# A first SwiGLU phase on [high | low] products, and four megabytes of modulation moved into the first mixer

## The chip, the cores and the metric

The program runs on one core of a Trainium2 chip as one launch. The metric is the device time of an execution in microseconds (us). The kernel before takes 1054.62 us as the median of three runs (1054.45 to 1054.63).

## The reference

A decoder trunk of two layers, one sequence of 256 tokens, width 1024, all in float32. Each layer has three sub-layers, each with RMSNorm and a modulation (shift, scale, gate) that is computed from a vector c:

```
mod = silu(c) @ ada_w[l] + ada_b[l]          # 1024 -> 9216: sh, sc, gt of the three sub-layers
x += 1/2 * gt1 * SwiGLU(mod(rms(x)), ffn1_w_in[l], ffn1_w_out[l])        # 1024 -> 2 x 2816 -> 1024
h  = mod(rms(x)); proj = h @ mix_w_in[l]
x += gt2 * concat(attention(8 heads x 64), conv(256 channels, 31 taps), GLA(4 heads x 64)) @ mix_w_out[l]
x += 1/2 * gt3 * SwiGLU(mod(rms(x)), ffn2_w_in[l], ffn2_w_out[l])
SwiGLU(h) = (silu(h @ w_a) * (h @ w_b)) @ w_out
```

At 256 tokens the block-sparse attention is plain causal attention over one block.

## The kernel before

The activations lie transposed in SBUF: 128 partitions of the feature dimension, 256 tokens along the free dimension. The weights stream from HBM once, 250 MB, by one DMA queue (SyncE's) in pieces of about 1 MB into a ring of five slots (`raw`). A slot is used again when both readers of it are done.

To keep float32 accuracy each operand is taken as a sum of a high and a low part in the type fp32r. `split` (L316) makes the parts of a weight piece: ScalarE casts the raw tile to `wh` (L330), VectorE subtracts to get `wl` (L333). A product is wh x high + wh x low + wl x high, and there are two ways to issue it. `mm3` (L360) uses three matmuls of 256 columns. `mm2` (L366) uses one matmul of 512 columns for wh against the neighbours [high | low] and one of 256 columns for wl against high; its two halves of the accumulator have to be added afterwards. `product` (L605 calls it) does a 256-column weight piece with `mm3`; both output halves fit one PSUM bank. `product2` does it with `mm2`; it takes two PSUM banks and ends with a ScalarE copy (L540) and a VectorE addition (L541) for each of them.

The six phases are (layer, part): (0, 0) the first SwiGLU, until about 225 us of the span; (0, 1) the first mixer, until about 348; (0, 2) the second SwiGLU; and the same for layer 1, whose mixer has about 738 to 860. In the kernel before only phase (0, 0) uses `product`, the later SwiGLU phases use `product2`.

The modulation weights are another 72 pieces of 1 MB on the same queue and ring. `PLAN` (L48) spreads them over the phases: for each phase (m, tensor, lo, hi), that is m steps while its weight pieces lo to hi are split, `tensor` of them on TensorE and the others on VectorE. `piece_done` (L350) issues them. A VectorE step is a multiply-add of a 128 x 2048 tile with one activation per partition (L229 for the first of a group, L231). A group of steps ends with a sum over partitions by four TensorE products (`ada_sum`, L250), a copy, and transposes and additions (`ada_finish`, L262, L267). `AT_END` gives a step on TensorE (L222) near the end of a phase.

The mixer multiplies W_in in pieces (L362 to L364, L722 to L724), forms the gate product of the linear attention (L801), runs the convolution's 31 taps on VectorE (L756), and attends two heads at a time in `attend` (L845), four times. One such block is: six score products (L852), masked maxima on VectorE (L860, L864), exponentials on ScalarE with their sums (L384), reciprocals on VectorE (L870), scaling on ScalarE (L872), six transposes of the probabilities on TensorE (L875), copies on ScalarE (L876), and the products with the values (L882). Then come the linear attention's state products (L932, the state S on VectorE L938 and L943, L947, L950), W_out for the attention and the other heads (L977 to L979 with split weights, L974 with raw ones), and the residual.

The order of each engine's instructions is not that of the text: a list scheduler sorts the whole program at build time by its own estimates of durations, and engines then run their queues in that order. Matmuls of weight pieces that are ready are so put under the latency of a softmax.

Of the kernel before, what the change touches and what calls it, by code (L numbers as in the profile page):

```python
# [8 lines left out]
F32 = mybir.dt.float32  # L9
# [3 lines left out]
AF = mybir.ActivationFunctionType  # L13
# [4 lines left out]
P = 128  # L18
T = 256
# [25 lines left out]
TAPS = (4, 2, 4, 4, 4, 4)  # L45
ORDER = (0, 2, 6, 4)

PLAN = {None: (0, 0, 0, 1), (0, 0): (22, 0, 0, 30), (0, 1): (0, 0, 0, 1), (0, 2): (19, 0, 5, 28), (1, 0): (15, 0, 5, 28),  # L48
        (1, 1): (0, 0, 0, 1), (1, 2): (4, 0, 2, 14)}
AT_END = {(0, 0): 1, (0, 1): 1, (0, 2): 1, (1, 0): 1, (1, 1): 0, (1, 2): 0}  # L50
HOOKS = {(0, 1): (0, 1), (0, 2): (0, 1), (1, 0): (0, 1), (1, 1): (0, 1), (1, 2): (0, 1)}
# [8 lines left out]
def trunk_kernel(ctx: ExitStack, tc: tile.TileContext, x, c, positions, ada_w, ada_b, ffn1_norm, ffn1_w_in,  # L60
# [4 lines left out]
    ACT, DVE, PE, POOL = nc.scalar, nc.vector, nc.tensor, nc.gpsimd  # L65
# [8 lines left out]
    def nm(s):  # L74
        uid[0] += 1
        return f"{s}_{uid[0]}"
# [5 lines left out]
    def unit(shape, dt=F32, s="u"):  # L82
        return u2.tile(shape, dt, tag="u2k", name=nm(s))
# [266 lines left out]
    def piece_done():  # L350
# [3 lines left out]
        ada_due(True)  # L354
        m, tensor, lo, hi = PLAN[state["phase"]]
        at = lambda x: m * min(max(x - lo, 0), hi - lo) // (hi - lo)
# [26 lines left out]
    def act(*args, **kw):  # L383
        chained(ACT.activation(*args, **kw).ins)  # L384
# [135 lines left out]
    def product(w):  # L520

        wh, wl = w
        o = halves(wide())
        for k in range(KD):
            for s in range(2):
                cs = P * s, P * s + P
                mm3(o[:, s, :], wh(k, *cs), wl(k, *cs), high(k), low(k), k + s == 0, k + s == KD)
        return o
# [35 lines left out]
    def ffn(l, i, w_in, w_out, done, first=None):  # L564
        begin(l, i)
        wi = w_in[l].rearrange("(k p) (ab f) -> p k ab f", p=P, ab=2)
        gT = []
        ws = []

        pairs = (l, i) != (0, 0)  # L570

        def piece(n, ahead=0):

            while len(ws) <= min(n + ahead, KF - 1):
                m = len(ws)
                ws.append(split(wi[:, :, m % 2, T * (m // 2):T * (m // 2) + T], [KD, T], fine=m < 2))
            return ws[n]

        state["ahead"] = piece
        def gated(a):  # L580
            for s in range(2):
                g = unit([P, 2 * T], F32R, "g")
                split_out(a[:, s, :], g)
                gT.append(g)

        if first is None:
            piece(1)
            pps = [[wide(), wide()] for _ in range(2)]
            opening(l, i, ws, pps, {HOOKS[l, i][0]: mean_square, HOOKS[l, i][1]: spread})
        else:  # L590
            open_ws, opened, bias, small = first
            ws += open_ws
        for ch in range(KF // 2):
            if (l, i) == (0, 0) and ch in (2, 6):
                next(tables_rope)
            if (l, i, ch) == (0, 2, 3):
                use_small(1, *load_small(1))
            if first is not None and ch == 3:
                use_small(0, *small)
            if first is not None and ch < 2:  # L600
                if ch == 0:
                    continue
                pb = product(piece(3))
                b = bias()
                for s in range(2):  # L605
                    act(opened[0][:, s, :], opened[0][:, s, :], AF.Silu, bias=b[:, s:s + 1])
                    DVE.scalar_tensor_tensor(opened[0][:, s, :], opened[1][:, s, :], b[:, 2 + s:3 + s],
                                             opened[0][:, s, :], op0=ALU.add, op1=ALU.mult)
                gated(opened[0])
                a = opened[2]  # L610
                for s in range(2):
                    act(a[:, s, :], a[:, s, :], AF.Silu, bias=b[:, 4 + s:5 + s])
                DVE.tensor_mul(a, a, pb)
            elif ch == 0:
                (a, ba), (b, bb) = rms(pps[0]), rms(pps[1])
                wh, wl = piece(2)
                pp = [wide(), wide()]
                for k in range(KD):
                    for s in range(2):
                        cs = P * s, P * s + P  # L620
                        mm3(pp[s][:, 0:T + 2], wh(k, *cs), wl(k, *cs), hT[:, k, 0, :], hT[:, k, 1, :], k == 0,
                            k == KD - 1)
                third = rms(pp)
                piece(3)
                modulated(l, i)
                for s in range(2):
                    act(a[:, s, :], a[:, s, :], AF.Silu, bias=ba[:, s, :])
                    DVE.scalar_tensor_tensor(a[:, s, :], b[:, s, :], bb[:, s, :], a[:, s, :], op0=ALU.add,
                                             op1=ALU.mult)
            else:  # L630
                if ch == 1:
                    a, ba = third
                    for s in range(2):
                        act(a[:, s, :], a[:, s, :], AF.Silu, bias=ba[:, s, :])
                elif pairs:
                    a = product2(piece(2 * ch))
                    act(a, a, AF.Silu)
                else:
                    a = unit([P, 2, T], F32, "ab")
                    act(a, product(piece(2 * ch)), AF.Silu)  # L640
                DVE.tensor_mul(a, a, (product2 if pairs else product)(piece(2 * ch + 1)))
            gated(a)
        wo = w_out[l].rearrange("(k p) n -> p k n", p=P)
        late = []
        for grp2 in range(4):
            pp = [wide(), wide()]
            for k0 in range(0, KF, 8):
                n = min(8, KF - k0)
                wh, wl = split(wo[:, k0:k0 + n, T * grp2:T * grp2 + T], [n, T])
                order = [(k, j) for k in range(n) for j in range(2)]  # L650
                if grp2 == 3 and k0 + n == KF:
                    order.sort(key=lambda t: t[1])
                for k, j in order:
                    g = gT[k0 + k]
                    mm2(pp[j], wh(k, P * j, P * j + P), wl(k, P * j, P * j + P), halves(g), k0 + k == 0, k0 + k == KF - 1)
                while late:
                    done(late.pop(0))
                if grp2 == 3 and k0 == 8:
                    ada(AT_END[l, i])
                    if done is not emit:  # L660
                        done.last()
            for j in range(2):
                for o in (pp[j][:, T:2 * T], pp[j][:, 0:T]):
                    residual(o, l, i, 2 * grp2 + j)
                if l == NL - 1 and i == 2:
                    late.append(2 * grp2 + j)
                else:
                    done(2 * grp2 + j)
        while late:
            done(late.pop(0))  # L670
# [545 lines left out]
```

## Time and profile before

| | before |
|---|---|
| median of three runs | 1054.62 us |
| the profiled execution | 1054.1 us, span 1052.4 us |
| granted TensorE clock, mean | 0.998 |
| TensorE busy | 1033.0 us, 98%, 6844 matmuls |
| VectorE busy | 848.7 us, 81% |
| ScalarE busy | 597.7 us, 57% |
| DMA | 251.40 MB, mean 239 GB/s |

The span is that of the profile, the execution's own time is 1.7 us longer. Busy shares are means over stages of different kinds; which engine limits a stage is read from the table of stretches, in which the busy time of an engine stands against the stretch's length, and from what TensorE waited for. Matmuls overlap, so the time of one is taken between the starts of many.

### The profile page before, as it was taken

How to read it: one execution, taken by the hardware profiler on the slowest of the kernel's cores; microseconds unless marked ns; L12 is line 12 of the kernel's file. 1: busy time of each engine (PE TensorE's matmuls, PEld its weight loads, DVE VectorE, ACT ScalarE, POOL GpSimd, SP SyncE). 2: the span in 40 equal slices, each digit the busy share in tenths (PEclk: the TensorE clock that was granted, in tenths of full speed). 3: DMA queues.
4: the chain of work that ended last, by engine and by line, in shares of the span. 5: the costliest groups of instructions: out<-in, count | busy, mean ns of one | idle time of the engine just before them, and what ended most of it. 6: DMA issues, size and time to landing. Idle time of an engine off the chain costs nothing.

```text
span 1052.4 us, 17429 instructions
## 1 busy us (share of the span) xinstructions
PE 1033.0 (98%) x6844; PEld 908.9 (86%) x6844; DVE 848.7 (81%) x1408; ACT 597.7 (57%) x1061; POOL 21.8 (2%) x58
## 2 busy tenths in 40 slices
PE   6999999999999999999999999999999999999998
PEld 5799998888888988888889888888879889888887
DVE  3798788879996899998669999866899779866652
ACT  4555454458667665564457555544767666555431
POOL 6000000001000000000000000000000000000000
PEclk9999999999999999999999999999999999999999
DMA  9999999985344679999666999867443455865430
GB/s 310 376 341 351 315 312 313 329 293 168 127 149 146 221 241 330 356 329 309 234 200 228 314 334 316 289 202 236 126 156 121 161 166 195 282 200 185 156 119 20
DMA packets 177638, 251.40 MB, mean 239 GB/s; under 512 B 7493, under 2 KB 156520, under 8 KB 170388
## 3 DMA queue, kind: packets, MB, share of 16 engines
q1 hardware_dynamic: 176480, 249.97, 70.5%
q8 instruction: 53, 0.87, 0.3%
q0 software_dynamic: 960, 0.28, 0.2%
q14 instruction: 29, 0.24, 0.1%
q10 hardware_dynamic: 116, 0.05, 0.0%
HBM read 249.23 MB, written 1.05 MB: 238 GB/s over the span
## 4 chain that ended last, share of the span: by engine, by line
PE 90%; ACT 3%; DVE 3%; DMA 3%; issue 0%; SPq 0%
PE mm L368 36%; PE mm L369 18%; PE mm L362 7%; PE mm L363 7%; PE mm L364 7%; PE mm L974 3%; PE mm L724 2%; PE mm L723 2%; PE mm L722 2%; DMA held<-in_ffn_w_in_dram 1%; ACT wh L330 1%; DMA adaraw<-in_ada_w_dram 1%; PE tp L222 1%; DVE wl L333 1%; PE tp L250 1%; DVE ab L756 1%
## 5 line engine op out<-in xcount | busy, mean ns | idle before, releaser
L333 DVE TENSOR_TENSOR wl<-raw,wh 128x1024 fp32r<-128x1024 f32 (+1 forms) x344 | 384.0, 1128 | 111.6 <-ACT wh L330 105.5
L330 ACT CAST wh<-raw 128x1024 fp32r<-128x1024 f32 (+1 forms) x344 | 330.9, 973 | 203.7 <-PE mm L368 100.9
L368 PE MATMUL mm<-hT,wh 128*128 128x512 f32 x912 | 322.8, 397 | 0.0
L369 PE MATMUL mm<-hT,wl 128*128 128x256 f32 x912 | 256.4, 282 | 0.0
L368 PE MATMUL mm<-g,wh 128*128 128x512 f32 x704 | 249.4, 398 | 0.0
L368 PEld LDWEIGHTS mm<-hT,wh 128*128 128x128 f32 x912 | 172.5, 189 | 43.0 <-DVE g L695 1.7
L369 PE MATMUL mm<-g,wl 128*128 128x256 f32 x704 | 197.6, 281 | 0.0
L362 PE MATMUL mm<-hT,wh 128*128 128x256 f32 (+1 forms) x656 | 188.4, 287 | 1.7 <-ACT wh L330 1.6
L363 PE MATMUL mm<-hT,wh 128*128 128x256 f32 (+1 forms) x656 | 187.2, 285 | 0.1
L364 PE MATMUL mm<-hT,wl 128*128 128x256 f32 (+1 forms) x656 | 186.6, 285 | 0.0
L369 PEld LDWEIGHTS mm<-hT,wl 128*128 128x128 f32 x912 | 171.8, 188 | 0.2
L368 PEld LDWEIGHTS mm<-g,wh 128*128 128x128 f32 x704 | 132.2, 188 | 35.0 <-ACT wh L330 2.5
L369 PEld LDWEIGHTS mm<-g,wl 128*128 128x128 f32 x704 | 133.0, 189 | 0.0
L362 PEld LDWEIGHTS mm<-hT,wh 128*128 128x128 f32 x656 | 125.2, 191 | 4.8 <-ACT wh L330 2.3
L231 DVE SCALAR_TENSOR_TENSOR adaacc<-adaraw,cact,adaacc 128x2048 f32<-128x2048 f32 (+1 forms) x59 | 123.5, 2093 | 3.9 <-DMA adaraw<-in_ada_w_dram 3.8
L363 PEld LDWEIGHTS mm<-hT,wh 128*128 128x128 f32 x656 | 124.9, 190 | 1.1 <-DVE hT L448 0.3
L364 PEld LDWEIGHTS mm<-hT,wl 128*128 128x128 f32 x656 | 124.9, 190 | 0.4 <-DVE wl L333 0.2
L540 ACT COPY ab<-mm 128x256 f32<-128x256 f32 x114 | 41.6, 369 | 51.5 <-PE mm L369 51.3
L546 DVE SCALAR_TENSOR_TENSOR xT<-mm,gate,xT 128x256 f32<-128x256 f32 x80 | 34.6, 478 | 25.1 <-PE mm L369 17.8
L756 DVE SCALAR_TENSOR_TENSOR ab<-hpad,cw,ab 128x256 f32<-128x256 f32 x120 | 51.0, 480 | 0.0
L541 DVE TENSOR_TENSOR ab<-ab,mm 128x256 f32<-128x256 f32 x114 | 46.3, 416 | 5.6 <-ACT ab L540 5.4
L724 PE MATMUL mm<-wl,hT 128*128 128x512 f32 (+1 forms) x128 | 47.5, 371 | 0.0
(225 smaller groups left out, 1051.4 us busy)
## 6 DMA issues: line engine op xcount, KB each, us to landing
raw<-in_ffn_w_in_dram SPq DMA_DIRECT2D x85, 1024.0 KB, 6.2
adaraw<-in_ada_w_dram SPq DMA_DIRECT2D x72, 1024.0 KB, 6.6
raw<-in_ffn_w_out_dram SPq DMA_DIRECT2D x32, 1024.0 KB, 5.6
raw<-in_mix_w_in_dram SPq DMA_DIRECT2D x24, 1024.0 KB, 5.4
raw<-in_ffn_w_out_dram SPq DMA_DIRECT2D x16, 768.0 KB, 6.0
raw<-in_mix_w_out_dram SPq DMA_DIRECT2D x8, 1024.0 KB, 5.0
held<-in_ffn_w_in_dram SPq DMA_DIRECT2D x12, 256.0 KB, 10.8
xn<-in_x_dram SPq DMA_DIRECT2D x2, 512.0 KB, 6.3
```

Source lines behind the costliest of these rows:

```text
L231: DVE.scalar_tensor_tensor(part, w, cact[:, k, 0:1], part, op0=ALU.mult, op1=ALU.add)
L330: ins = ACT.copy(hs[-1][:, b:c], raw(a + b, a + c)).ins
L333: DVE.tensor_sub(ls[-1][:, b:c], raw(a + b, a + c), f32(hs[-1][:, b:c]))
L362: PE.matmul(o, wh, high, start=first, stop=False)
L363: PE.matmul(o, wh, low, start=False, stop=False)
L364: PE.matmul(o, wl, high, start=False, stop=last)
L368: PE.matmul(halves(o), wh, pair, start=first, stop=False)
L369: PE.matmul(o[:, 0:T], wl, pair[:, 0, :], start=False, stop=last)
L540: ACT.copy(t[:, s, :], o[s][:, T:2 * T])
L541: DVE.tensor_add(t[:, s, :], t[:, s, :], o[s][:, 0:T])
L724: PE.matmul(pp[t][:, 0:n], a, wl(k, 0, n), start=False, stop=last)
L756: DVE.scalar_tensor_tensor(y[:, t, :], hpad[:, t, k:k + T], w, y[:, t, :], op0=ALU.mult, op1=ALU.add)
```

## The change

Two edits. All products of phase (0, 0) that used `product` use `product2` (19 of them: one in the second column group and 18 after it). And `PLAN` has 18 steps in (0, 0) in place of 22, and four in (0, 1), in its pieces 7 to 13.

```diff
--- before.py
+++ after.py
@@ -45,7 +45,7 @@
 TAPS = (4, 2, 4, 4, 4, 4)
 ORDER = (0, 2, 6, 4)
 
-PLAN = {None: (0, 0, 0, 1), (0, 0): (22, 0, 0, 30), (0, 1): (0, 0, 0, 1), (0, 2): (19, 0, 5, 28), (1, 0): (15, 0, 5, 28),
+PLAN = {None: (0, 0, 0, 1), (0, 0): (18, 0, 0, 30), (0, 1): (4, 0, 7, 13), (0, 2): (19, 0, 5, 28), (1, 0): (15, 0, 5, 28),
         (1, 1): (0, 0, 0, 1), (1, 2): (4, 0, 2, 14)}
 AT_END = {(0, 0): 1, (0, 1): 1, (0, 2): 1, (1, 0): 1, (1, 1): 0, (1, 2): 0}
 HOOKS = {(0, 1): (0, 1), (0, 2): (0, 1), (1, 0): (0, 1), (1, 1): (0, 1), (1, 2): (0, 1)}
@@ -567,8 +567,6 @@
         gT = []
         ws = []
 
-        pairs = (l, i) != (0, 0)
-
         def piece(n, ahead=0):
 
             while len(ws) <= min(n + ahead, KF - 1):
@@ -600,7 +598,7 @@
             if first is not None and ch < 2:
                 if ch == 0:
                     continue
-                pb = product(piece(3))
+                pb = product2(piece(3))
                 b = bias()
                 for s in range(2):
                     act(opened[0][:, s, :], opened[0][:, s, :], AF.Silu, bias=b[:, s:s + 1])
@@ -632,13 +630,10 @@
                     a, ba = third
                     for s in range(2):
                         act(a[:, s, :], a[:, s, :], AF.Silu, bias=ba[:, s, :])
-                elif pairs:
+                else:
                     a = product2(piece(2 * ch))
                     act(a, a, AF.Silu)
-                else:
-                    a = unit([P, 2, T], F32, "ab")
-                    act(a, product(piece(2 * ch)), AF.Silu)
-                DVE.tensor_mul(a, a, (product2 if pairs else product)(piece(2 * ch + 1)))
+                DVE.tensor_mul(a, a, product2(piece(2 * ch + 1)))
             gated(a)
         wo = w_out[l].rearrange("(k p) n -> p k n", p=P)
         late = []
```

Lines after the first edit stand up to five lower in the changed kernel: L870 there is L875 of before, L855 is L860, L972 to L974 are L977 to L979.

The scheduler sorts the first mixer anew; behind the mixer the order of all engines is the same as before. Two places of it follow. The first is TensorE's order at the fourth attention block of the first mixer. Before, W_out matmuls follow the last two score products; `mm_3725` and its neighbours are W_out accumulators, `wl_3732` and `wh_3731` the parts of a W_out piece, `mix` the heads' outputs:

```order
L852 MATMUL tp_3571<-qkT_2889,qkT_2887 128x128
L852 MATMUL tp_3570<-qkT_2889,qkT_2887 128x128
L979 MATMUL mm_3725<-mix_3236,wl_3732 128x256
L977 MATMUL mm_3725<-mix_3236,wh_3731 128x256
L978 MATMUL mm_3725<-mix_3236,wh_3731 128x256
L979 MATMUL mm_3725<-mix_3236,wl_3732 128x256
L979 MATMUL mm_3726<-mix_3236,wl_3732 128x256
```

Of such W_out matmuls 34 stand between the last score product and the first transpose (`tp_3590<-ident,tmp`). Now the same place, with `tp_3369` and `tp_3368` the scores of the two heads, `tmp` their probabilities, `wl_3530` and `wh_3529` the parts of a W_out piece:

```order
L847 MATMUL tp_3368<-qkT_2677,qkT_2676 128x128
L847 MATMUL tp_3369<-qkT_2678,qkT_2676 128x128
L847 MATMUL tp_3368<-qkT_2678,qkT_2676 128x128
L870 MATMUL tp_3388<-ident_70,tmp_2671 128x128 x3
L870 MATMUL tp_3405<-ident_70,tmp_2672 128x128 x3
L974 MATMUL mm_3523<-mix_3028,wl_3530 128x256
L972 MATMUL mm_3523<-mix_3028,wh_3529 128x256
L973 MATMUL mm_3523<-mix_3028,wh_3529 128x256
L877 MATMUL tp_3410<-tmp_2674,va_2679 64x256
```

The transposes follow the score products directly, and three W_out matmuls stand before the value products. The second place is VectorE's order around the same block. Before, W_out splits (`wl_3732`, `wl_3736`, `wl_3790`) stand ahead of the block's first maximum (L860); `acaus` belongs to the linear attention:

```order
L756 SCALAR_TENSOR_TENSOR ab_2742<-hpad_102,cw_19_113,ab_2742 128x256 x6
L333 TENSOR_TENSOR wl_3732<-raw_3729,wh_3731 128x1024
L333 TENSOR_TENSOR wl_3736<-raw_3729,wh_3735 128x1024
L695 TENSOR_TENSOR mix_3474<-tp_3469,mix_3474 128x256
L333 TENSOR_TENSOR wl_3790<-raw_3787,wh_3789 128x1024
L920 COPY_PREDICATED acaus_3554<-gmask_95,tp_3556 128x512
L920 COPY_PREDICATED acaus_3555<-gmask_95,tp_3557 128x512
L860 ISA tmp_2882,mx_3578<-tp_3570,amask_87 128x128
```

Now W_out's first splits (`wl_3530`, `wl_3534`) and the last of the four moved multiply-adds (`adaraw_3537`) stand behind the block's reciprocals, ahead of its output `mix` and of the linear attention's state `S`:

```order
L865 RECIPROCAL rin_3384<-rsum_3381 128x2
L751 SCALAR_TENSOR_TENSOR ab_2531<-hpad_102,cw_19_113,ab_2531 128x256 x2
L865 RECIPROCAL rin_3401<-rsum_3398 128x2
L333 TENSOR_TENSOR wl_3530<-raw_3527,wh_3529 128x1024
L333 TENSOR_TENSOR wl_3534<-raw_3527,wh_3533 128x1024
L231 SCALAR_TENSOR_TENSOR adaacc_2245<-adaraw_3537,cact_108,adaacc_2245 128x2048
L690 TENSOR_TENSOR mix_3415<-tp_3410,mix_3415 128x256
L933 COPY S_3440<-tp_3426 128x128
```

The other three multiply-adds stand on VectorE between the gate product and this block: behind the gate product, and ahead of the maxima of the first and of the third block. Between gate product and the fourth block's first maximum VectorE has three of them more, four splits of 128 x 1024 (L333) fewer and eight taps (L756) fewer than before. The four sums of the mixer's modulation group (L250) stood under the third block and now stand between the last raw W_out products.

## Rows read from the trace of the kernel before

**Rows 1.** Stretches (us from:to, length, busy time per engine, instructions, TensorE clock, DMA).

```profile
core 0: us, PE busy (x) PEld busy (x) DVE busy (x) ACT busy (x) POOL busy (x), PEclk, DMA share, GB/s
50.00:150.00 100.00, 100.00 (x832) 98.66 (x832) 87.64 (x114) 51.93 (x78) 0.54 (x1) 1.00 0.97 335
...
54.00:68.00 14.00, 14.00 (x116) 13.63 (x115) 13.97 (x26) 9.62 (x18) 0.00 (x0) 1.00 1.02 352
...
250.00:300.00 50.00, 49.55 (x302) 41.56 (x301) 49.15 (x114) 34.81 (x68) 2.94 (x6) 1.00 0.45 151
...
300.00:320.00 20.00, 18.96 (x164) 14.54 (x163) 18.88 (x54) 13.54 (x39) 0.00 (x0) 1.00 0.45 151
...
374.00:480.00 106.00, 106.00 (x609) 90.90 (x609) 101.81 (x131) 62.71 (x109) 0.00 (x0) 1.00 0.96 332
```

**Rows 2.** TensorE's waits from 225 to 348 us (total us, times, longest).

```profile
PE tp L875 <- ACT tmp L872: 1.0, 1, 1.0
PE tp L839 <- DVE tmp L834: 0.5, 1, 0.5
PE mm L974 <- DVE G L960: 0.3, 1, 0.3
```

**Rows 3.** Time line of TensorE, ends of two long stretches (start, duration, instruction).

```profile
67.77 0.39 PE L363 MATMUL mm<-hT,wh 128*128 128x256 f32 x1
...
124.02 0.28 PE L364 MATMUL mm<-hT,wl 128*128 128x256 f32 x1
...
480.07 0.40 PE L368 MATMUL mm<-g,wh 128*128 128x512 f32 x1
...
534.71 0.28 PE L369 MATMUL mm<-g,wl 128*128 128x256 f32 x1
```

**Rows 4.** VectorE's costs: costliest groups, time line at 106 us, groups in 250 to 300.

```profile
L541 DVE TENSOR_TENSOR ab<-ab,mm 128x256 f32<-128x256 f32 x114 | 46.3, 416 | 5.6 <-ACT ab L540 5.4
...
106.79 2.35 DVE L231 SCALAR_TENSOR_TENSOR adaacc<-adaraw,cact,adaacc 128x2048 f32<-128x2048 f32 x1
109.05 1.22 DVE L333 TENSOR_TENSOR wl<-raw,wh 128x1024 fp32r<-128x1024 f32 x1
...
L333 DVE TENSOR_TENSOR wl<-raw,wh 128x1024 fp32r<-128x1024 f32 x14 | 16.9, 1218 | 0.0
L756 DVE SCALAR_TENSOR_TENSOR ab<-hpad,cw,ab 128x256 f32<-128x256 f32 x38 | 16.4, 480 | 0.0
```

**Rows 5.** Time line of TensorE at the fourth block of the first mixer.

```profile
313.30 0.38 PE L979 MATMUL mm<-mix,wl 128*128 128x256 f32 x1
...
317.35 0.28 PE L978 MATMUL mm<-mix,wh 128*128 128x256 f32 x1
318.67 0.33 PE L875 MATMUL tp<-ident,tmp 128*128 128x128 f32 x1 [1.03 <-ACT tmp L872]
...
322.83 0.87 PE L882 MATMUL tp<-tmp,va 128*64 128x256 f32 x8
```

**Rows 6.** Time line of ScalarE and of VectorE at the same block.

```profile
314.02 2.18 ACT L330 CAST wh<-raw 128x512 fp32r<-128x512 f32 x4 [1.64 <-DMA raw<-in_ffn_w_in_dram]
316.11 0.49 ACT L384 ACTIVATE tmp<-tmp,nb,rq 128x128 f32<-128x128 f32 x1
...
314.08 0.28 DVE L860 CUSTOM_DVE_ANT_0 tmp<-tp,amask 128x128 f32<-128x128 f32 x1
```

**Rows 7.** Time line of TensorE at the first block: last scores over, first transpose.

```profile
282.89 0.38 PE L362 MATMUL mm<-hT,wh 128*128 128x256 f32 x1
...
286.96 0.33 PE L875 MATMUL tp<-ident,tmp 128*128 128x128 f32 x1
```

**Rows 8.** Time line of TensorE at a block of the second mixer.

```profile
815.79 1.53 PE L875 MATMUL tp<-ident,tmp 128*128 128x128 f32 x6 [0.32 <-ACT tmp L872]
818.14 0.87 PE L882 MATMUL tp<-tmp,va 128*64 128x256 f32 x8 [0.81 <-ACT tmp L876]
```

**Rows 9.** A stretch behind it (columns as in rows 1).

```profile
819.00:822.00 3.00, 3.00 (x24) 2.67 (x24) 2.81 (x4) 1.51 (x4) 0.00 (x0) 0.50 0.14 26
```

## The prediction

> **What bounds the kernel now.** I read the stretches first, then what TensorE waited for, then the time line of the places that the change touches. From 50 to 150 us, inside the first SwiGLU phase, TensorE is busy 100.00 of 100 us [rows 1]: nothing delivered sooner can help there, and only fewer or cheaper matmuls can. DMA is busy 0.97 of that stretch at 335 GB/s, but no TensorE wait comes from it. VectorE is the second tightest: 13.97 of 14 us in 54 to 68, and 49.15 of 50 us in 250 to 300, in the first mixer [rows 1]. The list of what TensorE waited for between 225 and 348 us has three entries of 1.0, 0.5 and 0.3 us [rows 2]; the reader should see that the mixer's softmax hardly shows, although it is a long chain VectorE, ScalarE, VectorE, ScalarE, TensorE. The time line says why. After the last score products of the fourth attention block, W_out matmuls start at 313.30 and run to 317.35, and the first transpose of the probabilities comes at 318.67 [rows 5]: 5.4 us of latency, 4.1 of them filled. The first block has 282.89 to 286.96, 4.1 us, all filled [rows 7].
>
> **The cheaper products.** A [high | low] product does per row of weights and half one 512-wide and one 256-wide matmul in place of three 256-wide. In this phase the 470 matmuls from 67.77 to the last at 124.02 take 56.25 us, 0.1198 each with a slower first one left out, so a triple is 0.359 us. In the W_out stretch of the second SwiGLU, from 480.07 to 534.71, there are 154 pairs and one wide matmul (0.23): 0.353 each [rows 3]. 19 products of 16 triples are 304: 304 x 0.006 = **-1.8 us**, all on TensorE's full stretch. It cannot be much more: 1.4 to 2.1 by the spread of such stretches.
>
> Each product adds two ScalarE copies and two VectorE additions (0.33 us each by starts, mean 0.416 [rows 4]), 38 additions or 12.5 us in all, while four multiply-adds leave the phase (2.26 us from 106.79 to the next start at 109.05 [rows 4], 9.0 together). VectorE so has 3.5 us more in some 110 us. In the full stretch 54 to 68 that is about 0.67 per product less one multiply-add in two or three products; the split of the next weights could fall up to 0.8 us behind. If so it is late on one side only and the queue of finished splits takes it. I put 0 there, up to 0.8. At the seam to the mixer the finish of a modulation group moves close ahead of the last W_out pieces, and the mixer's first operand may wait: **+0.2** (0 to 0.5).
>
> **The four moved megabytes.** They come as three VectorE multiply-adds before the fourth attention block's scores and one behind them, plus four slots of the raw ring. What moves with them is more than they are: the order of the changed program has no W_out product between the last scores of that block and its transposes, where before 34 stand; its W_out splits come on VectorE only behind the block's last reciprocal. So:
>
> - When do its scores reach VectorE? Between gate product and these scores VectorE gets three multiply-adds (2.3 each, 7.0) and loses four splits (1.218 each, 4.9) and eight taps (0.48 each, 3.8) [rows 4], 1.7 us less by means that overlap, about 0.9 by starts; the eight taps stand ahead of the gate product now and delay it. I take -0.5 (bounds -1 and +1.5). VectorE was full here, so it sets this moment, not TensorE.
> - From scores to first transpose: before, ScalarE does four weight casts (from 314.02) while VectorE has the maxima (from 314.08) and begins the exponentials only at 316.11 [rows 6]. In the changed order no cast stands there, so they can start at about 315.0: **-1.1**, chain 4.1 to 4.3 us like the first block's [rows 7]. Bounds -1.3 and 0.
> - TensorE work behind that first transpose: before, 58 W_out matmuls remain, now 88; 30 x 0.12 = 3.6, and the four 512-wide sums of the last modulation group (0.24 each, 0.9) fall behind it as well: **+4.5**. This is the counterpart of the missing cover: the work exists in both, but before it ran during the softmax, now TensorE idles for 4 us and does it afterwards.
> - Waits behind it. The second mixer shows a block without cover: transposes from 815.79, value products at 818.14 [rows 8], 2.35 us; the changed order has six transposes and three W_out matmuls there, some 0.75 of work, so 1.6 is waiting. Before, in this mixer, 318.67 to 322.83 [rows 5] was filled. Then the state copies: on VectorE two splits and one multiply-add (1.2 + 1.2 + 2.3) stand between the reciprocal and the copy of the state, so the products that read it wait some 0.6 us; queued behind the multiply-add are that copy, the state's decay and every later split. A slot of the raw ring that comes free later costs about 0.4. Together 2.6, less the 0.3 that TensorE waited behind this point before [rows 2]: **+2.3** (0.8 to 3.0).
>
> Mixer: -0.5 - 1.1 + 4.5 + 2.3 = **+5.2** (2 to 7.5).
>
> **The clock.** In the second mixer TensorE waited 0.32 us before 815.79 and 0.81 before 818.14, and the granted clock is 0.50 from 819 to 822 [rows 8, 9], its lower level of 1.2 GHz. In the first mixer a single wait of 1.03 us [rows 5] left the clock at 1.00 [rows 1]. The new idle stretch is four times that wait, and it is followed by the second one of the value products. At the lower level three microseconds hold 1.5 of work; the state wait of 0.6 would swallow part. I take **+0.7** (0 to 1.6). The Trainium skill, "TensorE: Matmul & The Clock Gate", section "HAM oscillation — how this bites in real kernels", says that idle gaps of TensorE between bursts bring the clock down and that the way back costs time; the second mixer's row agrees, the first mixer's shorter gap does not fall under it. By that rule the sum includes the 0.7, without it the sum is 0.7 less.
>
> **Sum.** -1.8 + 0.2 + 5.2 + 0.7 = +4.3. The profiled execution took 1054.1 us (span 1052.4 and 1.7 around it), so 1058.4; the median of the runs shown is 0.5 above the profiled one, hence **1058.9**. Behind the first mixer the order of all engines is unchanged, so nothing should be given back later; before 48 us it is unchanged too.
>
> **Rivals.**
>
> 1. Only the streaming counts: the fourth block comes early enough to make up for its missing cover. VectorE does less before its scores; if the gate product is not delayed and the three earlier blocks, which have more weight work under them, run without waits, the scores come some 4 us sooner, TensorE idles there, but everything behind it starts as early as before, and the 1.8 of waits that the mixer had [rows 2] go. Then the mixer ends about when it did, less the earlier opening: 1054.6 - 1.8 = **1052.9**, faster. It decides at scores that come some 4 us sooner after the mixer's opening than now. For it: DMA is at 0.45 in 300 to 320 [rows 1], so the raw tiles can be early, and the splits that leave the place before these scores are VectorE's. Against: VectorE's own sum gives 0.9 to 1.7, not 4.
> 2. The two nearly cancel: the mixer loses only 2 to 3 (low ends: scores -1, waits 0.8, no clock) and the time is **1054.9** to 1056. For it: each low end has a row; against: they must coincide.
> 3. Clock stays up: as forecast without 0.7 and with the lesser waits, **1057.5**.
> 4. VectorE falls behind in the first phase as well: the pairs need two accumulator banks per product and the additions free them; where VectorE is full (54 to 80 us) a product waits for a bank, and each of four or five products loses 0.4 to 0.6 us: +2.3, **1061.2**. For it 13.97 of 14; against: the same pairs fill 106.00 of 106 us from 374 on with VectorE at 101.81 [rows 1].
>
> **How the numbers follow.** Forecast with clock 0.44, rival 3 0.19, rival 4 0.07, rival 2 0.17, rival 1 0.13. A change under 0.2% (2.1 us: 1052.5 to 1056.7) is about what a measurement of this kernel can tell from none. Faster takes most of what lies below 1052.9 and its neighbourhood, 0.11; same is rival 2, the rest of rival 1 and the lowest part of rival 3, 0.23; slower the rest, 0.66. The range of 8 in 10 runs from 1053.6, which leaves out most of rival 1, to 1062.2, the forecast with mixer and clock at their high ends; the forecast's own range is 1056.8 to 1061.5.
>
> **What would show it.** Right: in the first phase pairs in the place of triples at 0.353 and no VectorE wait; the mixer opening 1.6 us earlier; in the fourth block TensorE idle for about 4 us with the releaser ScalarE's normalisation at the transposes, then ScalarE's copy of the transposed probabilities; a new wait before the state products put down to VectorE; granted clock 0.50 for some three microseconds behind it; the end of the mixer later by 4 and everything after it equal. Wrong: the fourth block's scores more than 2 us earlier relative to the mixer's opening, or waits for DMA in the mixer, or a loss of more than 1 us before 225 us.

## The result

The changed kernel takes 1060.93 us as the median of four runs (1060.41 to 1062.57), the kernel before 1054.53 us beside it: a ratio of 1.0059, 95% interval 1.0048 to 1.0071. It is 6.4 us slower; forecast were +4.3 us and 1058.9 us.

The profiled execution of the changed kernel took 1061.1 us, its span is 1059.4 us, 7.0 more than before. Where they lie is read from one row per phase, the statistic with which a phase opens (L462). These rows are of the time line of TensorE, first of before, then of after (start, duration, instruction):

```profile
33.92 0.49 PE L462 MATMUL tp<-ones,sqacc 128*128 128x1 f32 x3
...
229.01 0.39 PE L462 MATMUL tp<-ones,sqacc 128*128 128x1 f32 x3
...
351.36 0.47 PE L462 MATMUL tp<-ones,sqacc 128*128 128x1 f32 x3
```

```profile
33.28 0.61 PE L462 MATMUL tp<-ones,sqacc 128*128 128x1 f32 x4
...
226.90 0.50 PE L462 MATMUL tp<-ones,sqacc 128*128 128x1 f32 x4
...
358.17 0.58 PE L462 MATMUL tp<-ones,sqacc 128*128 128x1 f32 x4
```

The differences of such rows, for every run of this study, with the second mixer as the control (the other phases behind the first mixer, 194.5, 192.4 and 191.6, are the same within 0.4 us everywhere). The medians come from four chips, on which the kernel before took 1054.53 (the changed kernel), 1054.47 (e1 to e4), 1054.7 (e5 to e8) and 1055.08 us (e9 to e11); ratios below are to the kernel before on the same chip. One execution of e5 and one of the kernel before beside it, at 1262 and 1254 us with a mean clock of 0.76, belong to a slower state and are left out.

| kernel (profiled execution) | first SwiGLU | first mixer | second mixer | median us |
|---|---|---|---|---|
| before | 195.09 | 122.35 | 122.47 | 1054.5 |
| changed | 193.62 | 131.27 | 122.64 | 1060.93 |
| e1 pairs alone | 193.73 | 126.55 | 122.62 | 1056.17 |
| e2 plan alone | 194.62 | 132.42 | 122.37 | 1062.89 |
| e3 early window | 194.45 | 125.82 | 122.57 | 1057.21 |
| e4 filled | 193.61 | 129.40 | 123.73 | 1061.73 |
| e5 hoist, both mixers | 193.61 | 127.15 | 126.47 | 1063.29 |
| e6 pairs, casts held in both | 193.70 | 123.08 | 123.48 | 1053.67 |
| e7 as e6, and hoist in both | 193.81 | 123.49 | 125.36 | 1056.26 |
| e8 before, casts held | 195.09 | 122.84 | 121.84 | 1054.84 |
| e9 hoist, first mixer only | 193.61 | 126.51 | 122.54 | 1057.88 |
| e10 no TensorE step | 193.77 | 128.51 | 122.47 | 1059.64 |
| e11 pairs, casts held in the first | 193.75 | 123.07 | 122.63 | 1054.09 |

The first phase gained 1.5 us and the first mixer lost 8.9. TensorE's waits of the changed kernel from 223 to 358 us, which answer to [rows 2] (engine, line, what it waited for, total us, times, longest):

```profile
PE tp L870 <- ACT tmp L867: 3.8, 1, 3.8
PE tp L877 <- ACT tmp L871: 1.3, 1, 1.3
PE tp L222 <- DMA adaraw<-in_ada_w_dram: 0.7, 1, 0.7
PE tp L847 <- DVE acaus L915: 0.6, 1, 0.6
```

The second, 1.3 us, is at the value products of the first block (288.8 us). The longest is the fourth block without its cover. Its time line on TensorE, which answers to [rows 5]:

```profile
304.27 1.53 PE L870 MATMUL tp<-ident,tmp 128*128 128x128 f32 x6
306.47 1.04 PE L222 MATMUL tp<-adaraw,cact 128*32 128x512 f32 x2 [0.68 <-DMA adaraw<-in_ada_w_dram]
307.45 0.87 PE L877 MATMUL tp<-tmp,va 128*64 128x256 f32 x8
308.25 0.66 PE L904 MATMUL tp<-ident,ge 128*128 128x128 f32 x4
308.84 0.48 PE L910 MATMUL tp<-qt,G 64*128 64x128 f32 x2
309.25 1.05 PE L222 MATMUL tp<-adaraw,cact 128*32 128x512 f32 x4
...
310.67 1.05 PE L222 MATMUL tp<-adaraw,cact 128*32 128x512 f32 x2
...
314.00 0.93 PE L847 MATMUL tp<-qkT,qkT 64*128 64x128 f32 x10 [0.56 <-DVE acaus L915]
318.77 1.78 PE L870 MATMUL tp<-ident,tmp 128*128 128x128 f32 x6 [3.84 <-ACT tmp L867]
...
321.12 1.55 PE L877 MATMUL tp<-tmp,va 128*64 128x256 f32 x8
```

The reader should see two things. Between the scores' end (about 314.9) and 318.77 nothing runs. And between the third block's value products (307.45) and the fourth block's scores stand two groups of L222, the modulation step that TensorE does itself; another stands ahead of the value products and waits for its transfer. Before, the same step stood ahead of the third block's transposes and between them, and only the linear attention's products (L909, L915) lay between its value products and the scores:

```profile
306.13 1.04 PE L222 MATMUL tp<-adaraw,cact 128*32 128x512 f32 x2
...
310.04 0.87 PE L882 MATMUL tp<-tmp,va 128*64 128x256 f32 x8
...
312.43 0.94 PE L852 MATMUL tp<-qkT,qkT 64*128 64x128 f32 x12
```

From the value products to the scores' end it was 3.3 us before and is 7.5 us now. VectorE and ScalarE of the changed kernel at the same place, which answers to [rows 6]:

```profile
309.11 2.06 DVE L751 SCALAR_TENSOR_TENSOR ab<-hpad,cw,ab 128x256 f32<-128x256 f32 x5
313.22 1.34 DVE L915 COPY_PREDICATED acaus<-gmask,tp 128x512 f32<-128x512 uint32 x2 [2.05 <-PE tp L910]
...
315.24 0.28 DVE L855 CUSTOM_DVE_ANT_0 tmp<-tp,amask 128x128 f32<-128x128 f32 x1
...
316.19 0.49 ACT L384 ACTIVATE tmp<-tmp,nb,rq 128x128 f32<-128x128 f32 x1 [6.41 <-DVE nb L859]
```

VectorE sat idle for 2.05 us and waited for TensorE's products of the linear attention (L910), which stand behind the step; the last ten of the scores waited in turn for VectorE (L915). Before, VectorE came to the same copy without idle time:

```profile
312.84 1.35 DVE L920 COPY_PREDICATED acaus<-gmask,tp 128x512 f32<-128x512 uint32 x2
```

The clock falls in the idle stretch (columns as in [rows 1]; PEclk is the third figure from the end):

```profile
314.00:316.00 2.00, 0.93 (x10) 0.74 (x10) 2.00 (x8) 0.00 (x0) 0.00 (x0) 1.00 0.99 406
316.00:317.00 1.00, 0.00 (x0) 0.00 (x0) 1.00 (x8) 0.81 (x3) 0.00 (x0) 0.76 0.06 25
317.00:318.00 1.00, 0.00 (x0) 0.00 (x0) 1.00 (x4) 1.00 (x5) 0.00 (x0) 0.50 0.00 0
...
322.00:323.00 1.00, 1.00 (x22) 0.64 (x20) 1.00 (x1) 0.29 (x1) 0.00 (x0) 0.50 0.69 176
323.00:324.00 1.00, 1.00 (x24) 0.93 (x18) 0.88 (x4) 0.09 (x1) 0.00 (x0) 0.83 1.09 384
```

### The profile page after: what moved, and what is told of

Same layout as the page of the kernel before. It is cut to its first block, busy times and chain, and to the rows that moved or that the text cites. A ratio compares the mean times of both kernels' runs of the same rounds, so it can differ in the third digit from the quotient of the medians.

```text
span 1059.4 us, 16870 instructions
## 1 busy us (share of the span) xinstructions
PE 1035.5 (98%) x6540; PEld 894.6 (84%) x6540; DVE 860.7 (81%) x1446; ACT 610.5 (58%) x1099; POOL 21.9 (2%) x58
## 4 chain that ended last, share of the span: by engine, by line
PE 89%; DVE 6%; ACT 2%; DMA 2%; issue 0%; SPq 0%; ACTq 0%; DVEq 0%
PE mm L368 42%; PE mm L369 22%; PE mm L362 4%; PE mm L363 4%; PE mm L364 3%; PE mm L969 3%; DVE wl L333 2%; DMA adaraw<-in_ada_w_dram 1%; PE tp L222 1%; DVE ab L751 1%; PE mm L718 1%; PE mm L717 1%; PE mm L719 1%; PE tp L250 1%; PE mm L974 1%; PE mm L973 1%
## 5 line engine op out<-in xcount | busy, mean ns | idle before, releaser
L333 DVE TENSOR_TENSOR wl<-raw,wh 128x1024 fp32r<-128x1024 f32 (+1 forms) x344 | 383.4, 1127 | 109.7 <-ACT wh L330 103.5
L368 PE MATMUL mm<-hT,wh 128*128 128x512 f32 x1216 | 430.8, 397 | 0.0
L369 PE MATMUL mm<-hT,wl 128*128 128x256 f32 x1216 | 342.3, 282 | 0.0
L368 PEld LDWEIGHTS mm<-hT,wh 128*128 128x128 f32 x1216 | 229.9, 189 | 57.4 <-DVE g L690 1.7
L362 PE MATMUL mm<-hT,wh 128*128 128x258 f32 (+1 forms) x352 | 102.1, 291 | 1.6 <-ACT wh L330 1.6
L363 PE MATMUL mm<-hT,wh 128*128 128x258 f32 (+1 forms) x352 | 101.4, 288 | 0.0
L364 PE MATMUL mm<-hT,wl 128*128 128x258 f32 (+1 forms) x352 | 100.5, 286 | 0.0
L540 ACT COPY ab<-mm 128x256 f32<-128x256 f32 x152 | 55.1, 370 | 71.8 <-PE mm L369 71.5
L362 PEld LDWEIGHTS mm<-hT,wh 128*128 128x128 f32 x352 | 67.4, 192 | 3.4 <-ACT wh L330 1.9
L541 DVE TENSOR_TENSOR ab<-ab,mm 128x256 f32<-128x256 f32 x152 | 61.3, 417 | 9.7 <-ACT ab L540 9.4
L363 PEld LDWEIGHTS mm<-hT,wh 128*128 128x128 f32 x352 | 67.4, 192 | 0.9 <-DVE hT L448 0.2
L717 PE MATMUL mm<-wh,hT 128*128 128x512 f32 (+1 forms) x128 | 47.4, 370 | 0.0
```

The source lines that it names most:

```text
L333: DVE.tensor_sub(ls[-1][:, b:c], raw(a + b, a + c), f32(hs[-1][:, b:c]))
L362: PE.matmul(o, wh, high, start=first, stop=False)
L363: PE.matmul(o, wh, low, start=False, stop=False)
L364: PE.matmul(o, wl, high, start=False, stop=last)
L368: PE.matmul(halves(o), wh, pair, start=first, stop=False)
L369: PE.matmul(o[:, 0:T], wl, pair[:, 0, :], start=False, stop=last)
```

## The experiments

**e1, e2: the two halves of the change apart.** The edit of e1 is the changed kernel with the plan of before, that of e2 the kernel before with the changed plan. Of the line `PLAN` only the two entries that differ are shown:

```diff
# e1
-(0, 0): (18, 0, 0, 30), (0, 1): (4, 0, 7, 13)
+(0, 0): (22, 0, 0, 30), (0, 1): (0, 0, 0, 1)
```

Expected of e1: 

> The change's first half alone: products of the first SwiGLU phase by pairs, the plan of before (22 steps in the first phase, none in the first mixer). Theory A (the moved steps make the loss, through the order of the mixer that they bring): the fourth block keeps 36 W_out matmuls under its softmax, no wait over 1.5 us in the mixer, 1054.5 - 1.8 = 1052.7 us, bounds 1052.2 to 1053.5. Rival C (the pairs make the loss, through VectorE or a new order of everything): 1056 or more, with waits between 50 and 225 us or in the mixer.

Expected of e2: 

> The change's second half alone: triples in the first phase as before, 18 steps there and 4 in the first mixer. TensorE's order in the mixer is that of the changed kernel. Theory A: the whole loss of the mixer shows, 1054.5 + 8.2 = 1062.7 us (1061 to 1064), idle of 4 us in the fourth block, clock 0.50 behind it. Rival C: 1054 to 1056.

e1 took 1056.17 us, 1.0017 of before (1.0009 to 1.0026), e2 1062.89, 1.0073 (1.0059 to 1.0086). So the plan alone brings the mixer's loss, as theory A had it: e2 has the waits of 3.8, 1.3 and 0.6 us and a mixer of 132.42. But the pairs alone are 1.7 us slower where 1.8 faster was expected, which is what rival C had. Their phase gains 1.4 us as it should; the mixer grows by 4.2, with no modulation step moved, though the scheduler re-sorted some of its matmuls here too. TensorE waits twice in it, 1.6 us at the end of W_out for the linear attention's output and 2.2 us at the fourth block, which keeps the cover in the order, 36 matmuls, and yet waits. TensorE's row, then ScalarE's rows in e1:

```profile
318.45 0.33 PE L870 MATMUL tp<-ident,tmp 128*128 128x128 f32 x1 [2.16 <-ACT tmp L867]
```

```profile
312.52 2.18 ACT L330 CAST wh<-raw 128x512 fp32r<-128x512 f32 x4 [1.73 <-DMA raw<-in_ffn_w_in_dram]
314.61 0.49 ACT L384 ACTIVATE tmp<-tmp,nb,rq 128x128 f32<-128x128 f32 x1
...
316.95 1.14 ACT L330 CAST wh<-raw 128x512 fp32r<-128x512 f32 x2 [1.17 <-DMA raw<-in_ffn_w_in_dram]
318.00 0.80 ACT L867 ACTIVATE tmp<-tmp,rin 128x128 f32<-128x128 f32 x2
```

ScalarE's queue has casts of the next phase's weights between the exponentials and their scaling. Before, with the same order of ScalarE at this place, the cast came when its data was there, since everything ran 1.5 us later:

```profile
317.19 1.12 ACT L330 CAST wh<-raw 128x512 fp32r<-128x512 f32 x2
```

In e1 the exponentials in front of it end at 315.8 and the transfer at 316.95; the cast waits for it and the softmax waits behind the cast. After the 2.16 us of idle time the clock falls here too:

```profile
320.00:323.00 3.00, 3.00 (x16) 3.00 (x16) 2.76 (x10) 1.95 (x5) 0.00 (x0) 0.50 0.99 334
```

Together the halves cost 6.4 us, not 1.7 + 8.4: in the changed order no cast stands in the fourth block, so the pairs' own loss does not arise there.

**e3: the same four steps, earlier in the mixer.**

```diff
-(0, 1): (4, 0, 7, 13)
+(0, 1): (4, 0, 0, 6)
```

Expected: 

> The changed kernel with the four moved steps in the mixer's pieces 0 to 6 in place of 7 to 13: the same four megabytes, the same four VectorE multiply-adds in the same phase, but the scheduler leaves 29 W_out matmuls under the fourth block's softmax and 31 more matmuls under the first. Theory A (order): 1053.3 us (1052.5 to 1055), no wait of more than 1.5 us in the fourth block, clock 1.00. Rival B (the load of four more steps on VectorE and the queue in the mixer costs, wherever they stand): 1057 to 1061.

1057.21 us, 1.0027 of before (1.0017 to 1.0037). That is just inside rival B's range and outside A's, but the place of the loss is not B's: the fourth block waits only 1.0 us and the mixer is 5.4 us shorter than in the changed kernel, as A has it. What is left lies elsewhere: one of the moved steps has got into the chain of the mixer's norm. Rows of VectorE, then of TensorE, in e3:

```profile
231.65 0.15 DVE L395 TENSOR_TENSOR rs_t<-rs_t,rs_v 128x2 f32<-128x2 f32 x1
231.72 2.35 DVE L231 SCALAR_TENSOR_TENSOR adaacc<-adaraw,cact,adaacc 128x2048 f32<-128x2048 f32 x1
233.99 0.15 DVE L398 SCALAR_TENSOR_TENSOR rs_o<-rs_t,rs_y 128x2 f32<-128x2 f32 x1
```

```profile
238.61 0.58 PE L362 MATMUL mm<-hT,wh 128*128 128x256 f32 x1 [2.67 <-ACT hT L494]
```

The inverse root is a chain of operations of 0.15 us; a multiply-add of 2.3 us stands between its last two (and one split of 1.2 us more than before between the others), and TensorE waits 2.67 us at the end of that chain. The scores of the first block come 2.7 us later after the opening than before (55.7 against 53.0), so this place makes up most of the 3.5 us that the mixer lost. That the multiply-add alone is worth 2.7 was not tried; the step costs here by the place that it gets.

**e4: idle time filled, to keep the clock up.**

```diff
+            if l == 0 and pr == 3:
+                filled = bank()
+                products += [PE.matmul(filled[:, 0:T], hT[:, 0, 0, 0:P], hT[:, 0, 0, 0:T], start=True, stop=True)
+                             for _ in range(30)]
             row(products)
...
-                pT = bank()
+                pT = filled if s == 0 and filled is not None else bank()
```

Expected: 

> The changed kernel with 30 extra matmuls of 256 columns behind the last scores of the fourth block of the first mixer (their result is overwritten by the transposes): they fill 3.6 of the 4 us in which TensorE idled and give nothing. What is left of the idle time as such stays. If the lower clock costs time: granted clock 1.00 through 316 to 324 and 1060.9 - 1.2 = 1059.7 us (1058.9 to 1060.2). If the clock costs nothing there because ScalarE and VectorE pace the chain: 1060.9 within 0.4, at a clock of 1.00.

The clock stays at 1.00 and TensorE is busy in the former gap:

```profile
313.00:319.00 6.00, 5.37 (x48) 4.72 (x44) 5.60 (x22) 2.63 (x10) 0.00 (x0) 1.00 0.45 170
319.00:324.00 5.00, 4.86 (x55) 3.82 (x56) 5.00 (x6) 2.22 (x6) 0.00 (x0) 1.00 0.30 93
...
318.96 1.53 PE L875 MATMUL tp<-ident,tmp 128*128 128x128 f32 x6
```

The first mixer of this profile is 1.87 us shorter than the changed kernel's (129.40). Of that, 0.4 lie ahead of the transposes, where the step L222 waited 0.23 us for its transfer in place of 0.68. From the first transpose to the next opening it is 37.9 us (356.88 - 318.96) against 39.4: 1.5 less at the full clock, with 13 W_out matmuls also a little earlier in the order. e2 is a second row on the same question. All three engines have the changed kernel's order in its first mixer, but its clock is low until 329.0, not until 323.3:

```profile
320.21 1.09 PE L875 MATMUL tp<-ident,tmp 128*128 128x128 f32 x3 [3.84 <-ACT tmp L872]
...
319.00:329.00 10.00, 8.79 (x68) 6.78 (x68) 9.77 (x17) 4.72 (x13) 0.00 (x0) 0.50 0.55 182
```

From its first transpose (320.21) to the next opening (361.47) it takes 41.3 us, 1.9 more than the changed kernel.

The whole time of e4 does not show the gain: 1061.73 us (1060.60 to 1062.76), 1.0067 of before, above both ranges. The second mixer of its profile took 1.1 us more, with the order that it has in the changed kernel. There ScalarE's cast stood in front of the scaling and waited for its transfer, as in e1, and TensorE waited for the scaling, this time with the clock at 1.00 behind it:

```profile
832.35 1.14 ACT L330 CAST wh<-raw 128x512 fp32r<-128x512 f32 x2 [1.78 <-DMA raw<-in_ffn_w_in_dram]
833.84 0.33 PE L875 MATMUL tp<-ident,tmp 128*128 128x128 f32 x1 [2.20 <-ACT tmp L872]
834.00:841.00 7.00, 7.00 (x85) 6.15 (x84) 2.99 (x9) 5.27 (x13) 0.00 (x0) 1.00 0.96 307
```

So the price of the clock is about 1.5 us in one mixer of one profile, and not shown in the whole time.

**e5, e9: the cover given back.** The first W_out piece's fetch and split stand ahead of the fourth block in the text (e5 in both mixers, e9, whose edit is shown, only in layer 0); the plan and the work stay:

```diff
+        wo = mix_w_out[l].rearrange("(k p) n -> p k n", p=P)
+        early = split(wo[:, ORDER[0]:ORDER[0] + 2, :], [2, D]) if l == 0 else None
         attend(3)
...
-            w = (whole if k0 >= 4 else split)(wo[:, k0:k0 + 2, :], [2, D])
+            w = early if n == 0 and early else (whole if k0 >= 4 else split)(wo[:, k0:k0 + 2, :], [2, D])
```

Expected of e5: 

> The changed kernel with one piece of program text moved: the fetch and split of the first W_out piece stand ahead of the fourth attention block in place of behind it. Plan, pairs and all work are the same. The scheduler now puts its two VectorE splits and the fourth moved multiply-add ahead of the block and 29 W_out matmuls (and three sums) under its softmax. Theory A (the uncovered softmax and the clock behind it make most of the loss): the idle of 3.84 us goes below 1.2, granted clock 1.00, mixer shorter by 4 to 6: 1060.9 - 5 = 1055.9 us (1054.5 to 1057.5). Rival B (the four moved steps cost as load on VectorE and the queue): 1059.5 or more.

Expected of e9: 

> The hoisted run again, with the first W_out piece's fetch and split ahead of the fourth block in the first mixer only; in the earlier run the second mixer was hoisted too and grew by 4 us, which hid what the first one gained (131.27 to 127.15 us). Theory A: second mixer back at 122.5, first at 127.2: 1060.9 - 4.1 = 1056.8 us (1056 to 1057.8). Rival B (load of the moved steps): 1059.5 or more.

e5 missed, 1063.29 us, 1.0076 of before: it changed the second mixer as well, which had nothing to mend and grew by 4.0. e9 leaves that one alone and takes 1057.88 us, 1.0033 of before (1.0020 to 1.0045) on a chip where before took 1055.08: 2.8 above before in place of 6.4. That is at the upper end of A's range (1057.8) and below B's. The first mixer is 126.51, 4.8 us shorter than the changed kernel's: its transposes start 0.9 later after the opening, and from there to the next opening it is 33.8 us in place of 39.4. The wait at the fourth block's transposes is 0.81 and the clock stays at 1.00 through the mixer:

```profile
320.98 1.53 PE L870 MATMUL tp<-ident,tmp 128*128 128x128 f32 x6 [0.81 <-ACT tmp L867]
```

```profile
313.00:319.00 6.00, 5.99 (x58) 5.38 (x56) 6.00 (x23) 3.51 (x9) 0.00 (x0) 1.00 0.54 174
```

Theory A holds for over half of the mixer's loss, against rival B, with the same four steps in the same phase.

**e10: the modulation step on TensorE taken out of the mixer.** Only the entries that differ are shown:

```diff
-AT_END = {(0, 0): 1, (0, 1): 1,
+AT_END = {(0, 0): 1, (0, 1): 0,
-(0, 0): (18, 0, 0, 30)
+(0, 0): (19, 0, 0, 30)
```

Expected: 

> The changed kernel without the modulation step that TensorE does in the first mixer (four products of 512 columns twice, L222); that megabyte is a nineteenth VectorE step of the first phase, so nothing is left out. In the changed kernel these products stand between the third block's transposes and the fourth block's scores, outside any softmax, and the first of them waited 0.68 us for its transfer. If they made the scores late (3.7 us later after the opening than before): scores 2 to 3 us earlier, 1060.9 - 2.5 = 1058.4 us (1057.5 to 1059.3). Rival (VectorE sets the moment of the scores, as the prediction had it): scores at the same time, 1060.5 to 1061.5.

1059.64 us, 1.0045 of before (1.0031 to 1.0059), 4.6 above it in place of 6.4; by the bare time it is 0.3 above the expected range, by the distance to its own before inside it. The mixer is 2.8 us shorter:

```profile
312.40 0.93 PE L847 MATMUL tp<-qkT,qkT 64*128 64x128 f32 x10 [0.67 <-DVE acaus L915]
317.16 1.09 PE L870 MATMUL tp<-ident,tmp 128*128 128x128 f32 x3 [3.84 <-ACT tmp L867]
```

This mixer opens at 227.97, so the scores start 84.4 us after the opening, against 87.1 in the changed kernel (314.00 - 226.90): 2.7 us sooner. The wait of 3.84 is unchanged, so these are two separate losses. The scores still wait for VectorE's copy (L915), and start 1.0 us later than before (83.4).

**e6, e7, e8, e11: the casts held back.** ScalarE's casts of the next phase's first two pieces get an order behind the scaling of the fourth block's probabilities, without a semaphore:

```diff
                 ins = ACT.copy(hs[-1][:, b:c], raw(a + b, a + c)).ins
+                if fine and state.get("softmax") is not None:
+                    no_sync(ins, state["softmax"], "behind the softmax")
...
-                    ACT.activation(sc[:, a:b], sc[:, a:b], AF.Copy, scale=rin[:, h:h + 1])
+                    ins = ACT.activation(sc[:, a:b], sc[:, a:b], AF.Copy, scale=rin[:, h:h + 1]).ins
+                    if pr == 3:
+                        state["softmax"] = ins
```

Expected of e6, pairs with the plan of before: 

> Pairs in the first phase with the plan of before, and ScalarE's casts of the next phase's first two pieces held behind the scaling of the fourth block's probabilities (an order on ScalarE alone). In the run of the pairs alone one such cast waited 1.17 us for its transfer between the block's exponentials, TensorE idled 2.16 us and the clock fell to 0.50 from 320 to 323. Theory D (the mixer's loss of 4.2 us with pairs alone comes from these casts in ScalarE's queue: the faster first phase arrives at the block before the transfer): no wait over 1 us there, clock 1.00, 1056.2 - 3.2 = 1053.0 us (1052.3 to 1054). Rival: the casts are only late elsewhere, W_out's end or the next opening waits for them: 1055.5 to 1056.5.

Expected of e7, that with the hoist: 

> The same with the first W_out piece fetched and split ahead of the fourth block in the program text, as in the hoisted run. 40 matmuls under the fourth softmax, 2.7 us between its transposes and value products. If cover at this block is all that counts: 1052.7 us (1052 to 1053.8), the same or a little better than the held casts alone; if the splits in front of it delay the block's scores: up to 1 us worse.

Expected of e8, the kernel before with held casts: 

> The kernel before (triples, its plan) with the same holding of ScalarE's casts. There the casts delayed the exponentials by about 1 us and TensorE waited 1.03 us for them. Theory D: 1054.5 - 1.0 = 1053.5 us (1053.0 to 1054.2). Rival (what they were in front of has no room for them later): 1054.5 or more.

Expected of e11, e6 in the first mixer only: 

> Pairs in the first phase, the plan of before, and the holding of ScalarE's casts in the first mixer only; the second mixer is that of the kernel before. First phase 193.7, first mixer 123.1, the rest as before (122.4 to 122.6 in the second mixer): 1053.0 us (1052.4 to 1053.6), the fastest of the versions; if the second mixer's holding had no effect either way, 1053.7 as with both.

e6 takes 1053.67 us, 0.9989 of before (0.9980 to 0.9998): 1.0 below before on its chip, where e1 is 1.7 above. Its first mixer is 123.08, and the only wait in it is 1.4 us for the linear attention's output at W_out's end, which e1 has as well. e11 has the same first mixer and 1054.09 us, 0.9992 (0.9983 to 1.0001), on a chip where before took 1055.08; it is above its range and not faster than e6, though it leaves the second mixer alone (122.63 against 123.48). In its fourth block no cast stands in front of the scaling:

```profile
315.16 0.80 ACT L869 ACTIVATE tmp<-tmp,rin 128x128 f32<-128x128 f32 x2 [0.38 <-DVE rin L867]
```

So most of e1's loss goes with the casts: without them in front, the phase's 1.4 us remain, less 0.7 in the mixer. Of the 3.5 us between the first mixers of e1 and e6, 2.8 lie ahead of the fourth block's first transpose (91.3 and 88.5 us after the opening). (The scheduler moved some neighbours in the mixer along with them, so it is not one instruction alone that differs.) e7 missed (1056.26, 1.0011 of before): the first mixer gained nothing by the hoist (123.49), and the second is 1.9 longer than e6's and 2.9 longer than that of before. e8 missed as well, 1054.84, 1.0003 of before (0.9995 to 1.0012), no change: the 1.03 us of waiting at the block are gone, but TensorE waits 1.6 us at the end of W_out for the same output G that e6 waits for. There the rival was right.

## Why the prediction was right, and which step failed

The direction and the main mechanism held: the loss is in the first mixer, its largest wait is the fourth block's transposes for ScalarE's scaling, 3.84 us where "about 4" was forecast, and nothing is given back behind it. The time lies in the range. But the mixer lost 8.9 us where mixer and clock together had +5.9, so one step was wrong by more than its bounds, and the whole stayed in the range because the range left room for other terms. Step by step, in the profiled executions:

- **The cheaper products.** Forecast -1.8 and +0.2, so -1.6; measured 195.09 to 193.62, **-1.5**. A pair takes 0.353 us, as forecast (201 pairs from 68.00 to 139.01), no wait of TensorE stands between 48 and 225 us, so rival 4 did not occur. VectorE is busy 95.16 of 100 us in 50 to 150, in place of 87.64 [rows 1], and holds nothing up.
- **When the scores reach VectorE.** Forecast -0.5, bounds -1 to +1.5; measured: scores over 84.3 us after the opening before (313.30 - 229.01), 88.0 now, **+3.7**. This is the step that failed, in the words "it sets this moment, not TensorE". VectorE stood idle for 2.05 us there. Up to the third block's value products the changed kernel is 0.5 ahead (80.6 against 81.0 after the opening), much as forecast; the loss comes behind them. The prediction had counted that the sums L250 left their place under the third block, but not that the step L222 left it too and came to stand between that block and the next one's scores; its wait of 0.68 for a transfer is also the DMA wait in the mixer that the prediction had named as a sign of being wrong. e10 takes 2.7 of the 3.7 away.
- **From scores to first transpose.** Forecast -1.1; 5.37 to 3.84, **-1.5**.
- **Behind the first transpose.** Forecast +4.5 of work, +2.3 of waits and +0.7 of clock, 7.5 together; measured from there to the next opening 32.7 (351.36 - 318.67) to 39.4 (358.17 - 318.77), **+6.7**. From transposes to value products it is 2.35 us, as the second mixer had shown [rows 8]. The wait for the state did not appear as one: TensorE reached it late, at the lower clock.
- **The clock.** It is a part of those 6.7. It fell as forecast, but from 316.5 to 323.3 us, some 7 us where three were forecast. By e4 it is worth about 1.5 of the 6.7, inside the bounds, and work and waits are then about 5.2 in place of 6.8: the two errors offset each other, which is luck.

The sum of the first four is -1.5 + 3.7 - 1.5 + 6.7 = 7.4, and with the start before the first phase, which took 0.64 less, and 0.2 behind the mixer it is the 7.0 by which the spans differ.

Rival 1, only the streaming counts, had 1052.9 for it. It was to be decided by scores some 4 us sooner after the mixer's opening; they came 3.7 later. Nor are the pairs alone faster (1056.17). The prediction did not foresee that; it took the mixer of before as given for a faster first phase. The two fastest versions, e6 and e11, need both the pairs and a hand on ScalarE's order (e8 has that order without the pairs and gains nothing). Their gain over before, 0.1%, is at the edge of what the runs tell from none.

Which of the re-sorted mixer's smaller waits belong to which edit was not separated: e9 and e10 together would account for 7.5 of 8.9 us if they added, and they were not run together.

## What to carry to other kernels

Where a scheduler sorts the whole program, a change is worth what its order makes of it: count for each long chain (a softmax, a norm) which matmuls lie under it before and after, and for each engine what stands in its queue between two links of the chain. Work moved into a phase with such chains costs by its place: TensorE waited 2.67 us behind a chain of operations of 0.15 us into which a multiply-add of 2.3 us had come. A stage that gets faster brings the next stage to its transfers earlier; an instruction that waits for a transfer must not stand in front of one that others wait for.

## What the runs showed of the hardware

TensorE's granted clock went from 1.00 to 0.50 in or behind idle stretches of 3.84 us (changed kernel), 2.67 us (e3) and 2.16 us (e1). The length of one idle stretch does not settle it: the clock stayed at 1.00 behind 2.20 us (e4, second mixer), 1.62 us (e8, end of W_out in the first mixer) and 1.03 us (before). In the second mixer waits of 0.32 and 0.81 us were followed by a fall in the kernel before [rows 8, 9], and 0.45 and 0.82 us with the same order were not in e9:

```profile
819.00:826.00 7.00, 5.75 (x53) 4.42 (x54) 7.00 (x14) 4.51 (x12) 0.00 (x0) 1.00 0.12 37
830.53 0.33 PE L870 MATMUL tp<-ident,tmp 128*128 128x128 f32 x1 [0.89 <-ACT tmp L867]
```

What tells these cases apart is not shown. In the changed kernel the clock was back only at 323.3, some 4.5 us after TensorE had work again. Keeping TensorE busy with 30 useless matmuls held it at 1.00 (e4).

Nor has a fall one price. Behind the uncovered block it goes with 1.5 us (the changed kernel against e4), and some 4 us more of it behind the transposes with another 1.9 (e2). In the second mixer, with one order, it cost nothing that can be seen: with the fall 122.47, 122.64 and 122.47 us (before, changed, e10), without it 122.62, 122.37, 122.57 and 122.53 (e1, e2, e3, e9). Without the fall TensorE waited 0.9 us for ScalarE at the fourth block's transposes (the second row above, of e9); with it there was no wait there, so TensorE lost only time that it would have spent waiting.

The Trainium skill, "TensorE: Matmul & The Clock Gate", section "HAM oscillation — how this bites in real kernels", has idle gaps of TensorE as the cause of such falls. The fall in the 3.84 us and its absence in e4's filled gap agree in kind; the short waits of the second mixer, with a fall and without, are not told apart by it, and there the measurements decide.

The same order of the second mixer took from 122.37 to 122.64 us in the profiled executions of kernels that do not touch it, and 123.73 in e4 with the wait for a transfer, so a difference of 0.3 us in one mixer of one profile says nothing.
